# Dealing out the blocks of a tile: neighbouring 64 KB blocks at once instead of blocks further apart, in a 2 x 2 average pooling kernel

## The chip, the cores and the metric

The kernel runs on one core of one Trainium2 chip; the other cores are idle. The metric is the device time of one execution in microseconds (us). Ratios are made from fast runs alone, so they are not quite the ratios of the medians quoted. A kernel that was run once has no ratio, only its time.

## The reference

```
x: float32 (32, 128, 256, 256);  kernel_size 2, stride 2
output[:, :, i, j] = mean of x[:, :, 2i:2i+2, 2j:2j+2]      -> (32, 128, 128, 128)
```

1074 MB are read and 268 MB are written; a quarter of the input's size comes out, and there is almost no arithmetic.

## The kernel before

The input is seen as 524288 pooling rows of 512 numbers (two image rows side by side, 2 KB). A tile is 128 partitions x 32 pooling rows, so each partition (a row of the on-chip memory) gets one block of 64 KB of HBM, the chip's main memory, and gives one block of 16 KB back. The trace has one packet for each such block (16256 load packets of 64 KB, which is 127 tiles x 128). SP issues the loads and ACT the stores. Both kinds run on the same 16 DMA engines: of these engines' span the loads took 80.1% and the stores 20.1%, together all of it. VectorE (DVE) adds twice, ScalarE (ACT) scales by 0.25.

```python
    xv = x.rearrange("n c (ho a) w -> (n c ho) (a w)", a=2)
    ov = out.rearrange("n c ho wo -> (n c ho) wo")
    ins = [in_pool.tile([P, TILE, 2 * w], f32, name="in_tile") for _ in range(2)]     # TILE = 32
    res = [out_pool.tile([P, TILE, w_out], f32, name="res") for _ in range(3)]
    # ... semaphores cut ...
    xt = xv[0:whole * TILE * P].rearrange("(t p g) f -> t p g f", p=P, g=TILE)        # whole = 127
    ot = ov[0:whole * TILE * P].rearrange("(t p g) f -> t p g f", p=P, g=TILE)

    def load(t, b):
        sp.dma_start(out=ins[b], in_=xt[t]).then_inc(loaded[b], 16)

    def tile_sums(b):
        take(dve, stored[b], 16)
        take(dve, loaded[b], 16)
        sums(ins[b], res[b])

    def scale_store(t, b, landed):
        take(act, summed)
        act.sem_inc(free[b])          # SP may load this buffer again
        scale(res[b])
        take(act, scaled)
        act.dma_start(out=ot[t], in_=res[b]).then_inc(landed, 16)
    # ... the loops; the last tile is cut into four smaller parts ...
```

Partition p of tile t holds block 128t + p. By this pattern the HBM side of a load is one loop over 128 partitions (step 64 KB) and a contiguous run of 64 KB.

## Time and profile before

| | before |
|---|---|
| time, median of 3 runs | 3103.59 us (3103.52 to 3103.79) |
| span in the profile | 3101.5 us |
| moved | 1342.19 MB, 433 GB/s |
| DMA engines | 100% busy |
| DVE, ACT busy | 54%, 15% |

These lines are from the page of the kernel before: the span, the busy time of the engines (us, share, instructions), the GB/s of the DMA in 40 slices of the span, and the two DMA queues (loads on q1, stores on q10: packets, MB, share of the 16 engines' span).

```profile
span 3101.5 us, 2614 instructions
DVE 1679.6 (54%) x262; ACT 464.7 (15%) x132; POOL 0.2 (0%) x4
...
GB/s 416 436 440 426 436 440 426 437 440 424 438 440 423 439 437 425 440 428 434 440 433 430 442 423 436 439 427 440 435 426 437 439 427 436 438 424 439 437 425 416
...
q1 hardware_dynamic: 19008, 1075.85, 80.1%
q10 hardware_dynamic: 18720, 266.35, 20.1%
```

The two shares add up to all of the engines' time, so DMA is the bottleneck from end to end. The same lines give the time of one packet. The loads took 0.801 x 3101.5 x 16 = 39749 engine-us for 1075.85 MB, which is 2.42 us for 64 KB. The packet records of the trace agree and add the spread: the 16256 load packets of 64 KB took 2.418 us in the median, 2.418 at the 1st and 2.420 at the 99th percentile. The 16 KB store packets took 0.611 us. 64 KB in 2.418 us is 27.1 GB/s for one engine.

The issue part of the page and the timeline of one tile period show the slack (start, duration, engine, line, operation, and in brackets the idle time before it):

```profile
in_tile<-in_x_dram SPq DMA_DIRECT2D x127, 31.5
```

```profile
988.60 8.69 DVE L87 TENSOR_TENSOR in_tile<-in_tile 128x8192 f32<-128x8192 f32 x1 [10.92 <-DVEq L67]
997.44 4.43 DVE L89 TENSOR_TENSOR res<-in_tile 128x4096 f32<-128x4096 f32 x1
1002.05 3.62 ACT L97 ACTIVATE res<-res 128x4096 f32<-128x4096 f32 x1 [20.57 <-ACTq L67]
1002.21 0.33 SPq L84 DMA_DIRECT2D in_tile<-in_x_dram  x1
1005.90 0.34 ACTq L104 DMA_DIRECT2D out_dram<-res  x1
1012.79 8.69 DVE L87 TENSOR_TENSOR in_tile<-in_tile 128x8192 f32<-128x8192 f32 x1 [10.93 <-DVEq L67]
```

A load takes 31.5 us from issue to landing, longer than a tile lasts, so the next load is always queued. A tile starts every 24.2 us (988.60 to 1012.79), and DVE waits 10.9 us of that.

### The profile page before, as it was taken

To read this page: it belongs to the slowest core of one execution; us is meant where nothing else is said; L and a number is where in the kernel's file an instruction comes from. 1 tells how busy PE (TensorE), PEld (TensorE's weight loads), DVE (VectorE), ACT (ScalarE), POOL (GpSimd) and SP (SyncE) were. 2 spreads that over 40 slices of the span, in tenths; PEclk is the share of its full clock that TensorE was granted. 3 is DMA by queue.
4 is the path that set the end of the run, shared out by engine and by line. 5 is a ranking of instruction groups with operands and counts; after the bars stand their busy time and mean duration, and the time that the engine had idled before them with its cause. 6 is when DMAs were issued, how large, how long until landed. Compare 5 with 4: busy or idle time off the path is not lost. (4 is left out here: it accounts for less than half of the span.)

```text
span 3101.5 us, 2614 instructions
## 1 busy us (share of the span) xinstructions
DVE 1679.6 (54%) x262; ACT 464.7 (15%) x132; POOL 0.2 (0%) x4
## 2 busy tenths in 40 slices
DVE  4555555555555555555555555555555555555556
ACT  1111111111111111111111111111111111111111
POOL 0000000000000000000000000000000000000000
DMA  9999999999999999999999999999999999999999
GB/s 416 436 440 426 436 440 426 437 440 424 438 440 423 439 437 425 440 428 434 440 433 430 442 423 436 439 427 440 435 426 437 439 427 436 438 424 439 437 425 416
DMA packets 37728, 1342.19 MB, mean 433 GB/s; under 512 B 4192, under 2 KB 4192, under 8 KB 4576
## 3 DMA queue, kind: packets, MB, share of 16 engines
q1 hardware_dynamic: 19008, 1075.85, 80.1%
q10 hardware_dynamic: 18720, 266.35, 20.1%
HBM read 1073.74 MB, written 268.44 MB: 433 GB/s over the span
## 5 line engine op out<-in xcount | busy, mean ns | idle before, releaser
L87 DVE TENSOR_TENSOR in_tile<-in_tile 128x8192 f32<-128x8192 f32 (+1 forms) x131 | 1113.0, 8496 | 1396.4 <-DVEq L67 1396.4
L97 ACT ACTIVATE res<-res 128x4096 f32<-128x4096 f32 (+1 forms) x131 | 463.5, 3538 | 2594.8 <-ACTq L67 2594.8
L89 DVE TENSOR_TENSOR res<-in_tile 128x4096 f32<-128x4096 f32 (+1 forms) x131 | 566.8, 4327 | 19.2
L97 ACT ACT_TABLE_LOAD x1 | 1.3, 1283 | 36.3 <-ACTq L67 36.3
L234 POOL MEMSET const-bfloat16-1.0<- 128x1 bf16 x1 | 0.1, 101 | 0.0
L234 POOL MEMSET const-uint8-127<- 128x1 uint8 x1 | 0.1, 101 | 0.0
L234 POOL MEMSET const-float32-0.0<- 128x1 f32 x1 | 0.1, 98 | 0.2 <-issue 0.2
L234 POOL MEMSET const-float32-1.0<- 128x1 f32 x1 | 0.1, 98 | 0.0
## 6 DMA issues: line engine op xcount, KB each, us to landing
out_dram<-res ACTq DMA_DIRECT2D x126, 2048.0 KB, 30.8
in_tile<-in_x_dram SPq DMA_DIRECT2D x1, 4096.0 KB, 22.0
in_tile<-in_x_dram SPq DMA_DIRECT2D x1, 2048.0 KB, 27.1
in_tile<-in_x_dram SPq DMA_DIRECT2D x2, 1024.0 KB, 30.0
out_dram<-res SPq DMA_DIRECT2D x1, 2048.0 KB, 11.7
in_tile<-in_x_dram SPq DMA_DIRECT2D x127, 31.5
out_dram<-res ACTq DMA_DIRECT2D x1, 1024.0 KB, 8.1
out_dram<-res ACTq DMA_DIRECT2D x1, 512.0 KB, 6.0
```

The source lines that it names most:

```text
L87: dve.tensor_add(out=it[:, :, 0:w], in0=it[:, :, 0:w], in1=it[:, :, w:]).then_inc(halfway)
L89: dve.tensor_add(out=dst, in0=it[:, :, 0:w:2], in1=it[:, :, 1:w:2]).then_inc(summed)
L97: act.mul(out=dst, in_=dst, mul=0.25).then_inc(done)
L234: nc = _bacc.Bacc("TRN2", target_bir_lowering=False, num_devices=1)
```

## The change

The intent: let the 16 DMA engines read (and write) neighbouring blocks of HBM at the same time. The author takes it that engine e serves partitions 8e to 8e+7; that is an assumption. By it, engines before are at blocks 8 apart, 512 KB. After, partition 8e+j holds block 16j+e, so at step j all engines are within one megabyte.

```diff
     def block(r0, g):
         rows = slice(r0, r0 + g * P)
-        return xv[rows].rearrange("(p g) f -> p g f", p=P), ...
+        split = "(j e g) f -> e j (g f)"
+        return xv[rows].rearrange(split, e=16, g=g), ov[rows].rearrange(split, e=16, g=g)
+
+    def chip(tile):
+        return tile.rearrange("p g f -> p (g f)")
...
-    xt = xv[0:whole * TILE * P].rearrange("(t p g) f -> t p g f", p=P, g=TILE)
-    ot = ov[0:whole * TILE * P].rearrange("(t p g) f -> t p g f", p=P, g=TILE)
+    split = "(t j e g) f -> t e j (g f)"
+    xt = xv[0:whole * TILE * P].rearrange(split, j=8, e=16, g=TILE)
+    ot = ov[0:whole * TILE * P].rearrange(split, j=8, e=16, g=TILE)
...
-        sp.dma_start(out=ins[b], in_=xt[t]).then_inc(loaded[b], 16)
+        sp.dma_start(out=chip(ins[b]), in_=xt[t]).then_inc(loaded[b], 16)
...   (the stores and the parts of the last tile likewise)
```

The on-chip side stays 128 partitions of 64 KB. The HBM side can no longer be written as one loop. By the pattern it goes from one loop of 128 to two loops, 16 and 8:

```
before  HBM [step 64 KB, 128]                [64 KB in a row]
after   HBM [step 64 KB, 16] [step 1 MB, 8]  [64 KB in a row]
```

Below, "16 x 8" is this second form and "one loop" the first.

More of the change, by code (lines that the diff above doesn't have):

```diff
@@ L70, in block @@
         rows = slice(r0, r0 + g * P)
-        return xv[rows].rearrange("(p g) f -> p g f", p=P), ov[rows].rearrange("(p g) f -> p g f", p=P)
+        split = "(j e g) f -> e j (g f)"
+        return xv[rows].rearrange(split, e=16, g=g), ov[rows].rearrange(split, e=16, g=g)
+    def chip(tile):
+        return tile.rearrange("p g f -> p (g f)")
     whole, rest = divmod(units - 1, TILE)
     rest += 1
-    xt = xv[0:whole * TILE * P].rearrange("(t p g) f -> t p g f", p=P, g=TILE)
-    ot = ov[0:whole * TILE * P].rearrange("(t p g) f -> t p g f", p=P, g=TILE)
+    split = "(t j e g) f -> t e j (g f)"
+    xt = xv[0:whole * TILE * P].rearrange(split, j=8, e=16, g=TILE)
+    ot = ov[0:whole * TILE * P].rearrange(split, j=8, e=16, g=TILE)
     parts, a = [], 0
@@ L103, in scale_store @@
         take(act, scaled)
-        act.dma_start(out=ot[t], in_=res[b]).then_inc(landed, 16)
+        act.dma_start(out=ot[t], in_=chip(res[b])).then_inc(landed, 16)
     with tc.tile_critical():
@@ L123, in _pool_2x2 @@
         for a, b, part in parts:
-            sp.dma_start(out=it[:, a:b], in_=block((whole * TILE + a) * P, b - a)[0]).then_inc(part, 16)
+            sp.dma_start(out=chip(it[:, a:b]), in_=block((whole * TILE + a) * P, b - a)[0]).then_inc(part, 16)
         take(sp, held)
-        sp.dma_start(out=ot[whole - 1], in_=res[(whole - 1) % 2]).then_inc(tail, 16)
+        sp.dma_start(out=ot[whole - 1], in_=chip(res[(whole - 1) % 2])).then_inc(tail, 16)
         for b in range(2):
@@ L153, in _pool_2x2 @@
             take(act, scaled)
-            act.dma_start(out=block((whole * TILE + a) * P, b - a)[1], in_=dst[:, a:b]).then_inc(tail, 16)
+            act.dma_start(out=block((whole * TILE + a) * P, b - a)[1], in_=chip(dst[:, a:b])).then_inc(tail, 16)
         take(sp, tail, 16 * (len(parts) + 2))
```

## The prediction

> **What bounds the kernel now.** The 16 DMA engines. The page's slice table has DMA at 9 tenths in all 40 slices; the queue table gives 80.1% of the engines' span to the load queue and 20.1% to the store queue, together all of it. The page gives 1342.19 MB in a span of 3101.5 us, 433 GB/s. The table of stretches shows the same 433 to 434 GB/s at 200 to 1000, 1000 to 2000 and 2000 to 2900 us. DVE is busy 54%, ACT 15%; the groups view has DVE idle 1396 us waiting for loads, and the chain of waits gives the engines about 0%.
>
> The packet records of the trace say more. The 16256 load packets of 64 KB took 2.418 us each, and the 1st and 99th percentiles are 2.418 and 2.420 us; the 16 KB store packets took 0.611 us. So no packet ever waits on HBM: 64 KB in 2.418 us is 27.1 GB/s per engine, and 16 engines give 434 GB/s. [...] A tile costs an engine 8 x 2.418 + 8 x 0.611 = 24.2 us, and the timeline shows one tile every 24.2 us. Nothing is left over in the steady state.
>
> **What the change does.** It removes and adds no byte, no packet, no instruction and no wait. It changes only which HBM block goes to which partition: before, partition p holds block p; after, partition 8e+j holds block 16j+e. If engine e serves partitions 8e to 8e+7, the engines now read 16 neighbouring blocks of 64 KB at once, where they read blocks 512 KB apart. Partitions, descriptor sizes, DVE and ACT shapes stay. The HBM side of a transfer becomes 16 x 8 blocks instead of 128; issuing one costs 0.33 us today and has slack: loads are issued with another one still in flight (31.5 us from issue to landing for 19.3 us of load packets).
>
> **How much is on the critical path.** The whole DMA stream is, but the layout could only shorten stalls of HBM, and there are none to shorten. [...] What can still move is the ends: about 2.5 us of latency before the first landing (22.3 us after the start, of which 19.3 is packets) and a few us of last stores. An estimate: plus or minus 1 us.
>
> **Prediction.** 3103 us; 3098 to 3109 should hold it 8 times in 10. Faster by over 2%: 1%. Within 2%: 92%. Slower by over 2%: 7%.
>
> **What the profile would show.** Right: 64 KB packets still 2.42 us with no spread, 16 KB ones 0.61 us, 37728 packets, 433 GB/s, one tile every 24.2 us, DVE idle the same within a few us.
>
> **What would make it wrong.** (a) Neighbouring blocks may collide in HBM where distant ones did not: load or store packets would grow beyond 2.418 or 0.611 us, or spread out. (b) The 16 x 8 form of the HBM side may be cut over the engines differently, so that [...] engines finish unevenly: the 16 landings of one load, now within 1.0 us of each other, would spread. (c) It may be cut into smaller packets: the packet count would rise. Each makes it slower; I see nothing that makes it faster by 2%, since even all idle at both ends is under 0.3% of the span.

This forecast's sum: 8 x 2.418 + 8 x 0.611 = 24.2 us a tile, as before the change, so the time before, 3103 us, give or take 1 us for the ends.

## The result, and the profile after

| | before | after |
|---|---|---|
| time, median of 6 runs | 3103.60 us | 5402.85 us (5327.48 to 5482.71) |
| ratio of the fast runs | | 1.7218 (1.7178 to 1.7259) |
| 64 KB load packet, median (1st, 99th percentile) | 2.418 us (2.418, 2.420) | 4.404 us (3.939, 5.095) |
| 16 KB store packet, median | 0.611 us | 0.806 us |
| DMA engines busy | 100% | 100% |
| data packets, bytes | | the same |

The kernel is 72% slower. The time after splits into two groups, 5327 to 5353 us (fast) and 5453 to 5483 us (counted as slow); the ratio uses the three fast runs alone, and the profile shown is of a fast one. The granted clock is 1.0 in both groups, and what parts them is not known. The experiments below ran on four chips; the kernel before took 3103.3 to 3104.8 us on them. Single looks are compared with 5351 us, and no difference of a few per cent between slow kernels is given a reason.

The page after, the same lines:

```profile
span 5349.7 us, 2614 instructions
DVE 1680.0 (31%) x262; ACT 464.7 (9%) x132; POOL 0.2 (0%) x4
...
GB/s 224 244 241 248 246 245 246 248 247 245 246 247 246 249 250 253 252 253 254 255 255 254 255 255 253 253 251 253 254 254 254 256 256 257 254 256 257 258 257 256
...
q1 hardware_dynamic: 19008, 1075.85, 85.1%
q10 hardware_dynamic: 18720, 266.35, 14.9%
```

```profile
in_tile<-in_x_dram SPq DMA_DIRECT2D x127, 69.2
```

The instruction count is the same, the busy time of DVE and ACT is the same, and so are the packets and bytes of both queues. The engines are as busy as before, and move 251 GB/s in place of 433. So the packets themselves became slow: 0.851 x 5349.7 x 16 = 72842 engine-us for the same bytes, 4.44 us for 64 KB. A tile now costs 8 x 4.44 + 8 x 0.78 = 41.8 us of an engine (means of the packet records), and tiles land 41.7 us apart. "Busy" for a DMA engine therefore says nothing of its rate: 100% at 433 GB/s and 100% at 251.

How the slow packets begin is clearest before any store runs, between 5 and 40 us after the start. Two stretches of each kernel, before first (start:end, length, busy times of DVE, ACT and POOL, clock, DMA share, GB/s; a share a little over 1 comes from overlapping packets and packets counted whole at the edges):

```profile
5.00:40.00 35.00, 13.12 (x2) 3.65 (x2) 0.00 (x0) 1.00 1.04 449
2000.00:2900.00 900.00, 485.82 (x75) 133.79 (x37) 0.00 (x0) 1.00 1.00 434
```

```profile
5.00:40.00 35.00, 0.00 (x0) 0.00 (x0) 0.00 (x0) 1.00 1.02 210
2000.00:2900.00 900.00, 288.57 (x44) 79.55 (x22) 0.00 (x0) 1.00 1.00 254
```

In the opening the change runs at less than half the rate, and the packet records there come in groups of 16 that start within about 1.1 us of each other, at a median of 5.11 us a packet, 2.11 times 2.418.

### The profile page after: what moved, and what is told of

Read it like the earlier page. It is cut to its first block, busy times and chain, and to the rows that moved or that the text cites. A ratio compares the mean times of both kernels' runs of the same rounds, so it can differ in the third digit from the quotient of the medians.

```text
span 5349.7 us, 2614 instructions
## 1 busy us (share of the span) xinstructions
DVE 1680.0 (31%) x262; ACT 464.7 (9%) x132; POOL 0.2 (0%) x4
## 3 DMA queue, kind: packets, MB, share of 16 engines
q1 hardware_dynamic: 19008, 1075.85, 85.1%
## 6 DMA issues: line engine op xcount, KB each, us to landing
out_dram<-res SPq DMA_DIRECT2D x1, 2048.0 KB, 18.5
```

## The experiments

Three theories were on the table.

- **HBM**: neighbouring blocks collide in HBM where distant ones did not. It is about addresses.
- **PORT**: the 16 x 8 form makes an engine serve 8 partitions in a row, and engines then get in each other's way as they write into the on-chip memory. It is about which engine serves which partition. "Port" is a name for a way into that memory which some partitions would share. It is an assumption: no trace here shows a port, how many there are, or which partitions share one. So is it with the groups of 4 partitions. What the runs can show is how long packets take when the same bytes go to other sets of partitions, or in another form.
- **FORM**: something else about two loops on the HBM side slows an engine down, such as how the transfer is issued.

### 1. Form and address pulled apart

`grid_1mb` keeps the 16 x 8 form and takes the neighbours away: by assumption, an engine's 8 blocks lie side by side and the engines are 1 MB apart. (Tiles are made in pairs, so that the two loops can't be merged into one; the last two tiles' loads are one-loop.)

```diff
-    xt = ...rearrange("(t p g) f -> t p g f", p=P, g=TILE)
+    xs = ...rearrange("(T e s j g) f -> s T e j (g f)", s=2, g=TILE, e=16, j=8)   # tile t = 2T + s
```

> The 16 x 8 form of the HBM side kept, neighbours taken away: an engine's 8 blocks lie side by side, the engines 1 MB apart. Theory HBM (neighbouring blocks collide in HBM): collisions gone, 64 KB load packets back to 2.42 us, about 3105 us in all. Theory PORT (the 16 x 8 form makes each engine serve partitions 8e to 8e+7[...]): as slow as the changed kernel, load packets 4.2 to 5.1 us, 5200 to 5600 us in all, whatever the addresses.

Measured: 5363.94 us, correct; load packets 4.436 us in the median, 5.115 us in the opening. As slow as the change, without neighbours.

```profile
GB/s 224 245 245 246 244 245 246 247 247 246 246 248 247 249 247 250 249 248 251 252 254 256 253 254 253 250 250 252 253 251 252 251 251 252 252 251 250 252 253 300
```

The last slice, where the one-loop transfers of the end begin, is the only quick one.

`row_1mb` is its control: one loop, with partitions 128 KB apart. That puts engines 1 MB apart if each serves 8 partitions in a row, and 512 KB apart if they take groups of 4.

```diff
+    xs = ...rearrange("(T p s g) f -> s T p (g f)", s=2, g=TILE, p=P)
```

> Control of grid_1mb: engines 1 MB apart too, but the HBM side is one step for 128 partitions, as before the change (step 128 KB). PORT: 3104 us, load packets 2.42 us. HBM: 3104 us as well, unless a distance of 1 MB is bad in itself; then both this and grid_1mb are slow and the pair tells nothing.

Measured: 3103.60 us, ratio 0.9999 (0.9982 to 1.0016), load packets 2.418 us. The wider distance is harmless; whether it was 1 MB or 512 KB between engines the trace does not say.

`row_near8k` keeps neighbours and takes the form away: the 64 KB of a partition come as 8 pieces of 8 KB, dealt so that all partitions together cover one megabyte at a time.

```diff
+    xt = ...rearrange("(t k p g) f -> t p k (g f)", k=8, p=P, g=4)
```

> Neighbours kept, 16 x 8 form taken away: a partition's 64 KB come as 8 pieces of 8 KB, neighbouring partitions hold neighbouring pieces, one step for 128 partitions; all engines work within one 1 MB at a time, as in the changed kernel. Packets of 8 KB and 2 KB took 0.309 and 0.084 us before, so a tile costs 8 x 8 x (0.309 + 0.084) = 25.2 us and the estimate without collisions is 3220 us. PORT: 3150 to 3300 us. HBM: near the changed kernel, over 4500 us, 8 KB packets about 0.55 us.

Measured: 3175.29 us, ratio 1.0230 (1.0213 to 1.0247), with 8 KB packets at 0.309 us, the same as the few that the kernel before has. No collision shows. Smaller packets are the likely reason for the 2.3% (8 x 0.309 = 2.47 us for 64 KB, against 2.418): the estimate for them was 3220 us, 3.7% over the time before, so it was too high.

`row_slow_issue` is the kernel before with a quicker way of issuing a transfer turned off: an issue on SP takes 0.33 us in the kernel before, 0.49 us here and 0.56 us after the change. That the changed transfers are slow to issue for the same reason is the reading; the traces show the times alone.

```diff
+    nc.dge_precook = False
```

> The kernel before, with the quick way of issuing a transfer turned off, which the changed kernel's transfers do not get (its issue on ACT takes 0.55 to 0.65 us instead of 0.34). If the way of issuing were the cause: about 5400 us. PORT and HBM alike: 3104 us within 5, load packets 2.42 us, issue about 0.5 us.

Measured: 3104.04 us, load packets 2.418 us. The way of issuing is not the cause. Together the four runs speak against the addresses: slow goes with the 16 x 8 form. HBM as a cause falls with them, and again with `grid32x4` in part 3, which keeps the 64 KB neighbours themselves.

### 2. Fewer partitions in a transfer, without the 16 x 8 form

`halves64` takes the kernel before, addresses and one loop included, and cuts each load into two transfers of 64 partitions. That engines should hinder each other there was the assumption.

```diff
-        sp.dma_start(out=ins[b], in_=xt[t]).then_inc(loaded[b], 16)
+        for q in (0, 64):
+            sp.dma_start(out=ins[b][q:q + 64], in_=xt[t][q:q + 64]).then_inc(loaded[b], 16)
...
-        take(dve, loaded[b], 16)
+        take(dve, loaded[b], 32)
```

> The kernel before, each load cut into two transfers of 64 partitions (one step, no 16 x 8 form, addresses as before). [...] PORT: 64 KB load packets 4.2 to 5.1 us, about 5100 to 5500 us in all. Rival FORM (two loops on the HBM side make an engine slow in itself, no ports involved): 2.42 us and 3104 us.

Measured: 5468.79 us. Its stretches:

```profile
5.00:40.00 35.00, 0.00 (x0) 0.00 (x0) 0.00 (x0) 1.00 1.02 210
2000.00:2900.00 900.00, 275.47 (x42) 75.94 (x21) 0.00 (x0) 1.00 1.00 247
```

The opening is the change's to the digit (210 GB/s); packets took 5.12 us there, 4.49 in the median of the run.

`halves_g` is the control. It also cuts each load in two, but over all 128 partitions, half of each block at a time.

```diff
+        for g in (0, 16):
+            sp.dma_start(out=ins[b][:, g:g + 16], in_=xt[t][:, g:g + 16]).then_inc(loaded[b], 16)
```

> Control of halves64: each load again cut into two transfers, but each over all 128 partitions, with half of each block (32 KB). If cutting a load in two were what slowed halves64: about 5400 us. PORT: 3104 to 3115 us, 32 KB load packets 1.21 us as the kernel before shows for its one 32 KB load.

Measured: 3111.61 us. Cutting a load in two costs 8 us; cutting it so that each half goes to half of the partitions costs 2365 us.

`eighths16` uses eight transfers of 16 partitions (the wait in DVE goes up with the number of transfers here and below).

```diff
+        for q in range(0, P, 16):
+            sp.dma_start(out=ins[b][q:q + 16], in_=xt[t][q:q + 16]).then_inc(loaded[b], 16)
```

> The same with eight transfers of 16 partitions[...]. PORT: 64 KB load packets twice those of halves64, 9 to 10.2 us, and 9900 to 11500 us in all[...]. FORM: 3104 to 3200 us.

The sum behind this total, 9900 us, rested on a number of ports that no run shows.

Measured: 5839.57 us, a miss on the total. The opening was as expected, 9.23 us a packet (median of 64). Later packets fell to 4.96 us in the median of the run. The slices and the opening:

```profile
GB/s 130 147 176 212 229 230 248 238 240 235 223 200 232 236 225 230 207 223 240 240 238 240 241 237 247 238 255 243 254 248 251 241 233 232 239 247 245 241 232 252
```

```profile
5.00:40.00 35.00, 0.00 (x0) 0.00 (x0) 0.00 (x0) 1.00 1.06 120
```

So, in one-loop transfers, a 64 KB packet takes 2.42 us with 128 partitions in a transfer, 5.12 with 64 and 9.23 with 16. That engines hinder each other there is the reading; the runs show the packet times. The 5.12 and 9.23 us are read at the start; what makes packets quicker later is taken up in part 4.

### 3. Two loops with a shorter inner one

`grid32x4` is the change with one number different: the HBM side is 32 x 4, still two loops, still neighbouring 64 KB blocks. Partition 4q+i holds block 32i+q.

```diff
-    xt = ...rearrange(split, j=8, e=16, g=TILE)
+    xt = ...rearrange(split, j=4, e=32, g=TILE)        # ot and block() likewise
```

> The change with its HBM side as 32 x 4 instead of 16 x 8: still two loops on the HBM side, still neighbouring 64 KB blocks, but groups of 4 partitions[...] are whole in the outer loop. FORM: 5200 to 5600 us, as 16 x 8. PORT allows two outcomes: if an engine still gets 8 partitions in a row, 5200 to 5600 us; if the groups of 4 are dealt so that each engine keeps a port of its own, 3104 us, load packets 2.42 us, and then two loops on the HBM side are harmless.

Measured: 3103.29 us, load packets 2.418 us, correct. Repeated with timing as `grid32x4_timed`:

> The same kernel as grid32x4, now timed: neighbouring blocks at once[...]. If neighbouring blocks gain anything, or cost anything, in HBM: outside 3098 to 3109 us. PORT alone: equal to the kernel before within 0.1%, 3101 to 3106 us.

Measured: 3104.04 us (3103.37 to 3105.51), ratio 1.0002 (0.9989 to 1.0016). Its page:

```profile
q1 hardware_dynamic: 19008, 1075.85, 80.0%
q10 hardware_dynamic: 18720, 266.35, 20.1%
```

Against the 85.1% of a longer span after the change, this is the old picture again. FORM has fallen, and the intent of the change has had its fair trial: neighbouring blocks at once gain nothing and cost nothing.

`grid64x2` asks how the rule goes on (e=64, j=2 in the same place).

> The HBM side as 64 x 2, blocks again neighbouring. If the rule is that groups of 4 partitions must not be cut between the outer loop's 16 shares in a way that the inner loop crosses a group (16 x 8 does: its inner loop runs over 2 groups): 3104 us, load packets 2.42 us. If 32 x 4 was quick only because its inner loop is exactly one group of 4: 5200 to 5600 us.

Measured: 3103.82 us, load packets 2.418 us. So 64 x 2 is as harmless as 32 x 4. Inner loops of 2 and 4 cost nothing and one of 8 costs 72%; where between 4 and 8 the harm begins is not shown, since no other was tried with 16 engines.

`near_loads` and `near_stores` give the 16 x 8 form to the large loads or the large stores alone (the parts of the last tile keep it in both). Rows come out in another order, so both results are wrong.

```diff
-    ot = ...rearrange(split, j=8, e=16, g=TILE)                        # near_loads; near_stores: xt
+    ot = ...rearrange("(t p g) f -> t p (g f)", p=P, g=TILE)
```

> The change in its large loads alone; large stores as before (rows come out in another order, so the result is wrong on purpose). PORT: writes into the on-chip memory[...] carry nearly all of the loss: load packets 4.3 to 4.7 us, 5000 to 5400 us in all; store packets at 0.61 to 0.75 us.

Measured: 5514.35 us, above the expected 5000 to 5400; load packets 4.57 us, store packets 0.81 us in the median (expected 0.75 at most). The loads alone carry the whole loss, and slow the stores though these kept their old form. That the total exceeds the change's own (one run, 3% over 5351 us) is left without a reason.

> The change in its large stores alone, large loads as before (wrong rows on purpose). PORT: two store packets meet on a port only when both engines happen to be at a store, which is a fifth of their time; estimate: store packets 0.61 to 0.80 us, loads 2.42 us, 3104 to 3250 us in all. If stores through a shared port cost what loads do (x2.1): 8 x (2.42 + 1.28) = 29.6 us a tile, about 3790 us.

Measured: 3126.06 us, 0.7% above before; load packets 2.418, store packets 0.611 us in the median. Stores in the 16 x 8 form cost next to nothing here; most of the 0.7% falls at the end, where the parts of the last tile keep the form in their loads too: the last of 40 slices moved 330 GB/s, against 416 before, while the stretch from 2000 to 2900 us moved 432 against 434. Since stores took only 20.0% of the engines' span, two engines may seldom store at the same moment, so this does not say what stores that meet would cost.

### 4. Quick and slow packets within two loops, and the miss of `eighths16`

Up to here the link from 16 x 8 to `halves64` was only the same packet time (5.11 against 5.12 us). Two kernels set a quick and a slow two-loop transfer side by side. Both use about half of the engines' time in their opening, which has loads alone (a DMA share of 0.52 and 0.50). `grid8x4` cuts each load of grid32x4 into four transfers of 32 partitions, which would be 4 for each of 8 engines. `grid8x8` cuts each load of the change into two of 64 partitions, which would be 8 for each.

```diff
+        for q in range(4):           # grid8x4; grid8x8: range(2), 64 partitions each
+            sp.dma_start(out=chip(ins[b])[32 * q:32 * q + 32], in_=xt[t][8 * q:8 * q + 8]).then_inc(loaded[b], 16)
```

> grid32x4 with each load cut into four transfers of 32 partitions, HBM side 8 x 4: two loops, 8 engines at work, each share 4 partitions[...]. Theory PORT with shares in a row: [...]64 KB load packets 2.42 us; 8 engines carry 16 load and 8 store packets a tile, 16 x 2.42 + 8 x 0.61 = 43.6 us, about 5590 us in all. Rival (two loops of this kind slow an engine down in themselves): packets 4.4 to 5.1 us, 9600 us or more.

Measured: 5577.95 us, correct. Slow as a kernel, since half of the engines' time has no loads (the share of 0.52), but its packets are quick, 2.418 us (99th percentile 2.425):

```profile
q1 hardware_dynamic: 21040, 1075.86, 44.8%
```

That is 0.448 x 5576.2 x 16 engine-us for 1075.86 MB, 2.43 us for 64 KB: idle engines, not stuck ones.

> The changed kernel with each load cut into two transfers of 64 partitions, HBM side 8 x 8: 8 engines again, each share 8 partitions in a row if PORT is right[...]. PORT: load packets 4.5 to 5.1 us; [...]about 10500 us in all. If shares are not in a row but keep ports apart: 2.42 us and about 5590 us, as grid8x4.

The sum behind this total counted ports. It came to 82 us a tile, and so does one from what was measured: 16 load packets for each of 8 engines at the 5.12 us of halves64, an estimate.

Measured: 9396.17 us, correct; packets 5.07 us in the opening, as expected, and 4.34 in the median of the run, less than expected, so the total is 10% under the estimate:

```profile
q1 hardware_dynamic: 19008, 1075.85, 46.1%
```

That is 4.22 us for 64 KB by the same sum. About the same share of the engines' time in the opening, same on-chip bytes: what differs is the form, 8 x 8 against 8 x 4, and packets take 5.07 us in the opening in place of 2.418.

`same_ports` and `two_port_sets` were to settle the late relief of eighths16. From the third tile on, a load is eight transfers of 16 partitions x 16 KB, to two groups of partitions in turn (a quarter of the bytes, wrong). That the groups of `same_ports` share ports and those of `two_port_sets` don't was the assumption, which no run shows.

```diff
+        for g in range(0, TILE, 8):
+            for q in (0, 32):        # two_port_sets: (0, 16)
+                sp.dma_start(out=ins[b][q:q + 16, g:g + 8], in_=xt[t][q:q + 16, g:g + 8]).then_inc(loaded[b], 16)
```

> The kernel before, but from the third tile on a load is eight transfers of 16 partitions by 16 KB, to partitions 0-15 and 32-47 in turn[...] (a quarter of the bytes, a wrong result on purpose). [...]about 2430 us in all. If stores beside them are what relieved eighths16: below 2000 us.

The sum behind the 2430 us counted ports. It came to 18.5 us a tile, and so does one from what was measured: 2 MB a tile at the rate of the opening of eighths16, 16 packets of 64 KB in 9.23 us, an estimate.

Measured: 2864.64 us.

> The same with partitions 0-15 and 16-31 in turn[...]. If engines drift apart so that some are on one set while others are on the other: clearly faster than same_ports, towards the 13.3 us a tile that DVE needs, 1750 to 2200 us. If there is no drift: as same_ports, about 2430 us.

Measured: 2725.20 us. Both totals miss, and 5% between them is no verdict. The design was at fault, as the stretch of each shows (same_ports first):

```profile
2000.00:2900.00 900.00, 507.50 (x84) 142.30 (x43) 0.00 (x0) 1.00 0.86 188
```

```profile
2000.00:2900.00 900.00, 445.21 (x74) 123.56 (x37) 0.00 (x0) 1.00 0.69 166
```

The DMA engines are idle for 14% and 31% of that stretch: with a quarter of the bytes, loads, as I read it, wait for DVE in between and start together again, where eighths16 has a backlog throughout (share 1.00). Whether its engines drift apart and so hinder each other less, as I suppose, stays open. Its slices narrow this a little: the first store was issued at 96 us, yet the rate took some five slices of 146 us to climb from 130 to 229 GB/s. So what makes the packets quicker builds up slowly and does not come with the first stores.

## Why the prediction was wrong

Point by point:

- *The 16 DMA engines bound the kernel, at full packet rate.* Right: 2.418 us a packet before, and row_1mb, grid32x4 and grid64x2 can't get below it.
- *The layout could only shorten stalls of HBM, and there are none to shorten.* Right as far as it goes. That no packet waits on HBM was inferred from the packet time's lack of spread (2.418 to 2.420 us). In the 32 x 4 form, where packets kept their 2.418 us, neighbouring blocks gave 1.0002 of the time before (grid32x4_timed).
- *"It changes only which HBM block goes to which partition", "Partitions, descriptor sizes, DVE and ACT shapes stay."* This step failed. The change also rewrote the HBM side as 16 x 8, and with that form packets went from 2.418 to 5.11 us in the opening. I had granted the assumption that engine e serves partitions 8e to 8e+7, and took it to hold before and after alike. No trace shows which engine serves which partition, before or after. If 8 in a row is what makes packets slow, the assumption can't have held before, where they took 2.418 us with no spread, and after the change they behave as if it had become true. That is a reading.
- *What would make it wrong, (b): the 16 x 8 form is cut over the engines differently, the 16 landings of one load spread.* The sign came: the landings of one load spread over 16 us in the median, from 1.0. That the cut is behind it is the reading above. The chance of 7% was far too small, since the profile before could not exclude it and the change touched just that form. Its companions did not come: (a) no collision in HBM, (c) the same number of data packets.
- *Slack of the issue.* Right: a longer issue on SP costs nothing. It takes 0.33 us before, 0.49 us in row_slow_issue and 0.56 us in grid32x4, all three at 3103 to 3104 us.

The size can be followed. At the start 64 KB take 5.11 us, so the 8 load packets of a tile would take an engine 40.9 us if it stayed so. That is an estimate; the tiles came 41.7 us apart, though each engine also spends 8 x 0.78 = 6.2 us of a tile on stores. The likely reason is that while one engine stores, loads of another are hindered less, which would also be why load packets average 4.44 us and not 5.11. This last sentence is argued from these sums, not tested by a run.

What the runs show is narrower than PORT. The loss came with the loads alone (near_loads, 5514 us); it did not come from the addresses (row_near8k, grid32x4), the issue (row_slow_issue) or two loops as such (grid32x4, grid64x2); and packets were also slow where one-loop transfers went to 64 or 16 partitions (halves64, eighths16). "8 in a row" would not by itself explain those two, since 64 partitions over 16 engines are only 4 for each. The author's shared ports were meant to cover them and the change alike, but a port, and the engine of a packet, are in no trace.

## What to carry to other kernels

The shape in which a transfer is written can by itself make its packets slow, even where bytes, packets and partitions are unchanged (here 4.40 us in the median, from 2.418); the reading, which no trace shows, is that it decides which DMA engine serves which partition. Check the time of a packet after any such rewrite, since the engines show as busy either way (100% here, before and after). When packets already run at a constant minimum (here 2.418 us from the 1st percentile, 2.420 at the 99th), reordering addresses is unlikely to gain anything; it gained nothing here (1.0002 in grid32x4_timed). If blocks must be dealt out in two loops, try an inner loop of 4 or 2 first (32 x 4 and 64 x 2 were free, 16 x 8 cost 72%), and keep single transfers at 128 partitions (two of 64 took 5469 us here, eight of 16 took 5840).
